# Down-projection of a decoder block: two weight sums made in memory early on, one product added up on another's banks, last sums in another order

## The chip, the cores and the metric

The kernel runs on one core of a Trainium2 chip. The metric is device time in microseconds, the median of several executions. Beside it stands one execution taken by the hardware profiler, whose trace gives every instruction of the engines: TensorE (PE for its matmuls, PEld for its weight loads), VectorE (DVE), ScalarE (ACT), GpSimd (POOL) and SyncE (SP, which here only issues transfers).

## The reference

One layer of a hybrid decoder: attention and an RWKV-7 mixer, merged, then a gated MLP with a causal convolution. 512 tokens, width 1024, MLP width 2816, everything float32. The parts that matter here:

```python
def rwkv7_mixer(p_in, ...):
    ...
    def step(state, inp):
        r_t, w_t, k_t, v_t, a_t, b_t = inp
        sa = jnp.einsum('bhij,bhj->bhi', state, a_t)
        state = state * w_t[:, :, None, :] + sa[..., None] * b_t[:, :, None, :] + v_t[..., None] * k_t[:, :, None, :]
        return state, jnp.einsum('bhij,bhj->bhi', state, r_t)
    ...
def compress_blocks(kv, pe, w1, w2):
    ...
    return jax.nn.gelu(flat @ w1) @ w2
def conv_ffn(h, w_up, conv_w, conv_b, w_down):
    u = h @ w_up
    ...
    val, gate = jnp.split(c, 2, axis=-1)
    return (jax.nn.silu(gate) * val) @ w_down
```

## The kernel before, in words

The program is one long stream that keeps TensorE fed. Each fp32 product is made as three products of rounded parts: a weight tile `raw` is rounded by ACT to `whi` and the rest `wlo` is left by a subtraction on DVE (`wsplit`, L371). SP loads the weight tiles in a fixed order into three `raw` buffers (`wload`, L342).

The stages in order are these. **Preparation** (`prepare`, with `front`, `receptance` and `values_of` for the four pairs of heads) makes the RWKV vectors `kx`, `rx` and `vx`. Then come the query and key projections. The **recurrence** is a loop over eight chunks `c` of 64 tokens. In each chunk PE makes `X`, DVE copies it to `Xs` (L1101), PE makes `U`, ACT and DVE copy it to `UV`, and PE makes `M` and `Y`. Between these small steps the loop calls `next(fill)`: `fill_chain` puts dense products there, and the pieces of `compress`, the two small MLPs on compressed keys and values. Those MLPs need the weights `cmp_w1`, read in four steps `s4`; some of their blocks are loaded by POOL (`spent_load`, L869 and L871) into tiles that the recurrence has finished with: step 2 into `AB` of chunk 0, step 3 into `BKT` of chunk 0 and `AR` of chunk 1. `compress` also clears the tile `vcb` on POOL (a part of `kc`, L969) before ACT writes into it, norms its result with `kcs` on DVE, and scales `kcd` (a part of `QK`), which PE then transposes (L989). In the loop the order on PE was written by hand. The scheduler ordered the other engines, POOL among them.

After attention, output projection and up-projection comes the **down-projection**, in which the order on all engines is written by hand. It multiplies 2x2 blocks in the Strassen-Winograd way, with seven products P1 to P7 on eight banks of PSUM. The rows of `w_down` come in eleven pairs `g`; a pair has four blocks B11 and B12 (loaded as `b1`), B21 and B22 (as `b2`). Four sums of them are needed, and DVE makes them in place: `sum_13` makes B11+B12 and B12+B22 in `b1`, and `sum_24` makes from these the two in `b2`. Even pairs are loaded by POOL into `cgq` (L1773), odd ones by SP into `raw`. Each sum is then split by ACT (`sum_hi`) and DVE (`sum_lo`). P2 and P1 come first, with weights as they are. Then a loop over the pairs makes P5, P7, P4 and P6; P6 takes over the banks of P1 after ACT has copied them to `u[0]`. Last comes P3, during which DVE adds up the results and stores them, four steps and then the two `ends`, each step needing one more split of a weight tile (`produce`).

Of the kernel before, what the change touches and what calls it, by code (L numbers as in the profile page):

```python
# [10 lines left out]
F32 = mybir.dt.float32  # L11
# [73 lines left out]
def hybrid_block(ctx: ExitStack, tc: tile.TileContext, A: dict, out: bass.AP):  # L85
# [14 lines left out]
    dp = ctx.enter_context(tc.tile_pool(name="dram", bufs=1, space=DRAM))  # L100
    wp = ctx.enter_context(tc.tile_pool(name="w", bufs=1))
    usum = dp.tile([4, 512, 128 * len(SF)], F32, name="usum")

    def pool(name, side="left"):
        cm = tc.tile_pool(name=name, bufs=1, side=side)
# [131 lines left out]
    def sums_in_memory(lead=3):  # L237
# [4 lines left out]
        for n in range(len(todo) + lead):  # L242
# [5 lines left out]
            if n >= lead:  # L248
# [2 lines left out]
                                    up_rows(*src, k) if type(src) is tuple else usum[src][128 * k:128 * k + 128],  # L251
                                    accum_op=ALU.add, max_dma_last_dim=2048)

    def weight_tiles():
        def cols(w, o, kt=KT, eng=v):
            return w[:, o:o + 128], kt, 128, eng

        def rows(w, o, n, kt=KT, eng=v):
            step = 1024 // n
            for i, k0 in enumerate(range(0, kt, step)):  # L260
                kn = min(step, kt - k0)
                yield w[128 * k0:128 * (k0 + kn), o:o + n], kn, n, eng[i] if type(eng) is list else eng

        def down_rows(e, c0, order=DOWN):
            src = A["w_down"][0].rearrange("(g e p) n -> e p g n", e=2, p=128)[e]
            for gs in order:
                yield src[:, gs[0]:gs[-1] + 1, c0:c0 + 512], len(gs), 512, v

        pool_ = nc.gpsimd
        yield cols(w_in, O_RWKV + 1536, eng=pool_)  # L270
        yield cols(w_in, O_RWKV + 1664, eng=pool_)
        for p in range(NH2):
            for o in (512, 0, 1024):
                yield cols(w_in, O_RWKV + o + 128 * p)
        yield cols(w_in, O_KC)
        yield from rows(w_in, O_Q, 512, eng=[v, pool_, ("spare", pool_), v])
        yield cols(w_in, O_VC)
        yield from rows(w_in, O_KS, 256, eng=[v, ("spare", v)])
        for m in range(NGA):
            yield cols(w_in, O_GA + 128 * m)  # L280
        yield from rows(w_in, O_KW, 280, eng=pool_)
        for m in range(NGA, KT):
            if m == NGA:
                yield A["cmp_w1_k"][0][0:512], 4, 256, None
                yield A["cmp_w1_v"][0][0:512], 4, 256, None
            elif m < 4:
                yield A["cmp_w1_v"][0][512 * m:512 * m + 512], 4, 256, None
            yield cols(w_in, O_GA + 128 * m)
        for m in range(NGB):
            yield cols(w_in, O_GB + 128 * m)  # L290
        for m in range(KT):
            if m + NGB < KT:
                yield cols(w_in, O_GB + 128 * (m + NGB))
            yield cols(A["w_proj_b"][0], 128 * m, NH2)
        for m in range(KT):
            yield cols(A["w_proj_a"][0], 128 * m, NH2)
        yield from rows(A["w_out"][0], 0, 512)
        yield from rows(A["w_out"][0], 512, 512, eng=())
        for f in range(SF[0]):
            yield cols(A["w_up"][0], DFF + 128 * f)  # L300
            yield cols(A["w_up"][0], 128 * f)
        stream = []
        for f in list(SF) + [None]:
            p = SF[-1] if f is None else f - 1
            if f is not None:
                stream += [up_block(f, 0, 0), up_block(f, 1, 0)]
            if f != SF[0]:
                stream.append(up_sum(p, TS4))
            if f is not None:
                stream.append(up_sum(f, TS2))  # L310
            if f != SF[0]:
                stream.append(up_block(p, 1, 1))
            if f is not None:
                stream += [up_sum(f, TS1), up_sum(f, TS3)]
        yield stream[:1], 4, 128, v
        for i in range(1, len(stream) - 2, 2):
            yield stream[i:i + 2], KT, 128, v
        yield cols(A["w_up"][0], DFF + 128 * (SF[-1] + 1))
        yield stream[-2:], KT, 128, v
        for f in range(SF[-1] + 1, NF):  # L320
            if f != SF[-1] + 1:
                yield cols(A["w_up"][0], DFF + 128 * f)
            yield cols(A["w_up"][0], 128 * f)
        yield from down_rows(1, 0)
        yield from down_rows(0, 0, DOWN_)
        for g in range(1, NG, 2):
            yield A["w_down"][0][256 * g:256 * g + 128], 1, D, "sum"
            yield A["w_down"][0][256 * g + 128:256 * g + 256], 1, D, "sum"
        yield from down_rows(1, 512)

# [245 lines left out]
    def front(p):  # L576
        kx = t2("kx", 2)
        shift_mix(dense_fm(hh, hl), 4 + p, kx)
        L[p]["kx"] = kx

    def rates(p):
        cs = slice(128 * p, 128 * p + 128)
# [39 lines left out]
    def receptance(p):  # L622
        rx = t2("rx", 2)
        shift_mix(dense_fm(hh, hl), p, rx)
        L[p]["rx"] = rx

    def values_of(p):
        vx = t2("vx")
        shift_mix(dense_fm(hh, hl), 8 + p, vx)
        L[p]["vx"] = vx  # L630

    def values_tok(p):
        vx = L[p]["vx"]
# [76 lines left out]
                yield  # L710

    steps = prepare()
    with tc.manual_schedule(engines={mybir.EngineType.PE}):
        next(steps)
        kcp = dense_fm(hh, hl)
    run(steps)
# [369 lines left out]
                mm(U[hsl(r), 64 * p:64 * p + 64], AB[hsl(r), c, p, r, 0:64], Xs[hsl(r), p], True, True)  # L1086
                yield

    with tc.manual_schedule(engines={mybir.EngineType.PE}):
        M0 = Ys = gn = None  # L1090
        X = pb()
        run(x_own(0, X))
# [1 line left out]
        for c in range(NCH):  # L1094
# [4 lines left out]
                spent_load(3, 0)  # L1099
            Xs = tp.tile([128, NH2, DH], F32, name="Xs", tag="Xs", bufs=2)  # L1100
            v.tensor_copy(Xs, X[:, 0:256].rearrange("p (a d) -> p a d", d=DH))  # L1101
            next(fill, None)
            U = pb()
            if c < NCH - 1:
# [630 lines left out]
    ring = xr.tile([128, 2, 2, 2, 512], F32R, name="ring", tag="hl2")  # L1735
    sraw = cgq[:, 0:8].rearrange("p (r a) n -> p r (a n)", r=2)

    def product(banks, x, w, first=False, end=False, ts_=(0, 1)):

        for n, (x_, y) in enumerate(((x[0], w[0]), (x[1], w[0]), (x[0], w[1]))):  # L1740
            for t in ts_:
                mm(banks[t], x_[:, 128 * t:128 * t + 128], y, first and n == 0, end and n == 2)

    def res(t, c, n=512, c0=0):
        return x1[:, t, 512 * c + c0:512 * c + c0 + n]
# [19 lines left out]
    def sum_load(g):  # L1765
        if g >= NG:
            return
        if g % 2:
            raws[g] = [loads.pop(0)[0][:, 0] for _ in range(2)]
        else:  # L1770
            raws[g] = [sraw[:, i] for i in range(2)]
            for i in range(2):
                nc.gpsimd.dma_start(raws[g][i], A["w_down"][0][256 * g + 128 * i:256 * g + 128 * i + 128])  # L1773

    def sum_13(g):
        if g < NG:
            b1, b2 = raws[g]
            tt(b1[:, 0:512], b1[:, 0:512], b1[:, 512:1024], ALU.add)
            tt(b1[:, 512:1024], b1[:, 512:1024], b2[:, 512:1024], ALU.add)

    def sum_24(g):
        if g < NG:
# [26 lines left out]
    with tc.manual_schedule(engines=everything):  # L1809
# [4 lines left out]
        for i, gs in enumerate(DOWN):  # L1814
            w = ahead.pop(0)
            produce()
            if i == 4:
                reload(0, 0, nc.sync)
            elif i == 5:
                sum_13(0)  # L1820
            for j, g in enumerate(gs):
                product(P2, split[N2][g], [x[:, j] for x in w], g == 0, g == NG - 1)
        for i, gs in enumerate(DOWN_):
# [3 lines left out]
            if i == 0:  # L1827
                h13 = sum_hi(0, 0)
                sum_24(0)
            elif i == 1:  # L1830
                h24 = sum_hi(0, 1)
                T[0] = [sum_lo(0, 0, *h13)]
            elif i == 2:
                T[0].append(sum_lo(0, 1, *h24))
                sum_load(2)
            elif i == 3:
                two_parts(a2a[:, 0, :, 0], a2a[:, 1, :, 0], ql[:, 0:5])
            elif i == 4:
                two_parts(a2b[:, 0, :, 0], a2b[:, 1, :, 0], ql[:, 5:NG])
            elif i == 5:  # L1840
                add_to(0, 0, P2)
                sum_load(1)
                sum_13(1)
            for j, g in enumerate(gs):
                product(P1, (a1[:, 0, g], a1[:, 1, g]), [x[:, j] for x in w], g == 0, g == NG - 1)
        u = [[ql[:, 4 * k + 2 * t:4 * k + 2 * t + 2].rearrange("p a n -> p (a n)") for t in range(2)] for k in range(3)]
# [1 line left out]
        for g in range(NG):  # L1848
            n, last = g + 1, g == NG - 1
            if not last:  # L1850
                if g == 0:
                    act_copy(u[0], P1)
                    P6 = [pa(), pa()]
                h13 = sum_hi(n, 0)
                sum_24(n)
                h24 = sum_hi(n, 1)
# [13 lines left out]
                if g == NG - 2:  # L1870
                    two_parts(a1[:, 0, 3:5], a1[:, 1, 3:5], ql[:, 14:16])
                    two_parts(a1[:, 0, 5:7], a1[:, 1, 5:7], cgq[:, 8:10])
                sum_13(g + 2)
            else:
                produce()
                produce()
# [2 lines left out]
            for p, x, w in ((P5, D1, t1), (P7, D3, t3))[::-1 if last else 1]:  # L1879
                product(p, split[x][g], w, g == 0, last)  # L1880
            product(P4, A22p[g], t4, g == 0, last)
            product(P6, split[N2][g], t2, g == 0, last)
        act_copy(u[2], P7)
        add_to(1, 0, u[2])
        add_to(1, 1, u[2], ALU.subtract)
        P3 = [pb(), pb()]
        for i, gs in enumerate(DOWN[:-2]):
            w = ahead.pop(0)
# [2 lines left out]
            if i == 0:  # L1891
                add_to(1, 0, P4)
            elif i == 1:
                for t in range(2):
                    tt(u[0][t], u[0][t], P6[t], ALU.add)
                add_to(1, 0, u[0], eng=nc.gpsimd)
            elif i == 2:
                for t in range(2):
                    tt(u[1][t], u[0][t], P5[t], ALU.add)
            elif i == 3:  # L1900
                store(1, 0, nc.sync)
            produce()
        add_to(0, 1, u[1], ALU.subtract)
# [40 lines left out]
```

## Time and profile before

| | us |
|---|---|
| median of 3 runs | 801.0 (800.76 to 801.12) |
| profiled execution, device time | 801.39 |
| its span in the trace | 799.6 |
| PE, PEld busy in the span | 788.0, 669.3 |
| DVE, ACT, POOL busy | 643.7, 484.6, 93.1 |
| recurrence, first `Xs` to last | 175.60 to 265.78 |
| loop over pairs in the down-projection, first matmul | 718.93 |
| P3, first and last matmul | 779.17 and 795.34 |

The device time is 1.8 us more than the span. Times in the trace count from the start of the span. A matmul's end is modelled, so two matmuls overlap in the rows, and where PE is held up is better read from the distance between starts than from busy time.

### The profile page before, as it was taken

Reading aid. Unit: us, or ns where it says so; the run is one execution under the profiler, and the core shown is the slowest. Engines: PE = TensorE matmul, PEld = TensorE weight load, DVE = VectorE, ACT = ScalarE, POOL = GpSimd, SP = SyncE. Lnnn points to the kernel's source line nnn. Section 1 sums busy time; section 2 is a strip of 40 time slices with the busy share of each in tenths; the row PEclk is TensorE's granted clock in tenths of the full one; section 3 lists DMA queues with packets and bytes.
Section 4 is the critical chain, followed back from the end, with each engine's and each line's share of the span. In section 5 each row is a group of like instructions: output and inputs, shape, how many; then the busy total and the mean of one; then the engine's idle time right before and its main releaser. Section 6 shows DMA issues by size and latency. Waiting matters only on the chain.

```text
span 799.6 us, 14331 instructions
## 1 busy us (share of the span) xinstructions
PE 788.0 (99%) x5475; PEld 669.3 (84%) x5475; DVE 643.7 (80%) x1184; ACT 484.6 (61%) x935; POOL 93.1 (12%) x126
## 2 busy tenths in 40 slices
PE   7999999999999999999999999999999999999997
PEld 5788888887777887887888888999999888888885
DVE  4688899974565688788675489888898999889997
ACT  6777765554455678777435366777777754553452
POOL 5300021152000052221000100000000000002101
PEclk9999999999999999999999999999999999999999
DMA  7432323337362289999757824666666322685754
GB/s 222 125 86 73 99 70 110 82 106 210 81 127 59 73 235 256 267 261 275 180 201 237 190 106 133 185 185 184 185 183 181 112 80 80 196 300 168 237 173 151
DMA packets 141081, 129.17 MB, mean 162 GB/s; under 512 B 5885, under 2 KB 121780, under 8 KB 140884
## 3 DMA queue, kind: packets, MB, share of 16 engines
q1 hardware_dynamic: 125360, 84.00, 36.7%
q0 software_dynamic: 14592, 41.71, 19.8%
q10 hardware_dynamic: 1060, 2.55, 1.0%
q8 instruction: 43, 0.70, 0.4%
q14 instruction: 26, 0.21, 0.1%
HBM read 122.79 MB, written 31.65 MB: 193 GB/s over the span
## 4 chain that ended last, share of the span: by engine, by line
PE 95%; DVE 2%; ACT 2%; DMA 1%; issue 0%; DVEq 0%
PE ps_mm L125 61%; PE ps_mm L1626 9%; PE ps_a L125 8%; PE ps_b L125 5%; PE ps_b L1626 4%; PE ps_a L1626 2%; PE ps_b L1357 1%; PE ps_mm L1357 1%; ACT P L128 1%; ACT whi L128 1%; DMA kc<-in_consts_dram 1%; DVE raw L131 1%; DVE wlo L371 0%; PE ps_b L409 0%; PE ps_b L668 0%
## 5 line engine op out<-in xcount | busy, mean ns | idle before, releaser
L128 ACT ACTIVATE whi<-raw 128x1024 fp32r<-128x1024 f32 (+2 forms) x150 | 149.3, 996 | 128.3 <-PE ps_mm L125 56.4
L371 DVE TENSOR_TENSOR wlo<-raw,whi 128x1024 fp32r<-128x1024 f32 (+1 forms) x135 | 154.7, 1147 | 42.7 <-ACT whi L128 25.1
L125 PE MATMUL ps_mm<-hh,whi 128*128 128x512 f32 (+1 forms) x416 | 161.5, 391 | 0.3 <-ACT whi L128 0.2
L125 PE MATMUL ps_mm<-hl,whi 128*128 128x512 f32 (+1 forms) x416 | 154.2, 382 | 0.0
L125 PE MATMUL ps_mm<-hh,wlo 128*128 128x512 f32 (+1 forms) x416 | 103.9, 382 | 0.0
L125 PEld LDWEIGHTS ps_mm<-hh,whi 128*128 128x128 f32 x416 | 78.2, 188 | 17.7 <-issue 0.8
L125 PEld LDWEIGHTS ps_mm<-hh,wlo 128*128 128x128 f32 x416 | 78.1, 188 | 15.5 <-DVE wlo L371 0.3
L125 PEld LDWEIGHTS ps_mm<-hl,whi 128*128 128x128 f32 x416 | 76.2, 188 | 14.5 <-DVE hl L140 0.3
L1773 POOL DMA_DIRECT2D cgq<-in_w_down_dram x12 | 6.4, 537 | 289.1 <-DVE cgq L131 236.5
L128 ACT ACTIVATE P<-P,nm 128x512 f32<-128x512 f32 (+3 forms) x64 | 35.3, 553 | 6.5 <-DVE nm L1320 6.4
L131 DVE TENSOR_TENSOR cgq<-cgq 128x512 f32<-128x512 f32 (+1 forms) x49 | 32.8, 670 | 1.6 <-DMA cgq<-in_w_down_dram 0.8
L140 DVE SCALAR_TENSOR_TENSOR cgq<-cr,cw,cgq 128x511 f32<-128x511 f32 (+1 forms) x38 | 28.4, 748 | 5.4 <-ACT cgq L128 5.0
L1320 DVE CUSTOM_DVE_ANT_0 P<-ps_a,AB 128x512 f32<-128x512 f32 (+3 forms) x64 | 29.3, 483 | 2.6 <-PE ps_a L125 2.6
L140 DVE SCALAR_TENSOR_TENSOR cgq<-ps_mm,cw,cgq 128x511 f32<-128x511 f32 (+1 forms) x36 | 26.2, 742 | 0.8 <-ACT cgq L128 0.7
L1626 PE MATMUL ps_mm<-hl,whi 128*128 128x256 f32 x104 | 26.1, 283 | 0.0
L1626 PE MATMUL ps_mm<-hh,whi 128*128 128x256 f32 x104 | 26.1, 283 | 0.0
L128 ACT ACTIVATE ring<-cgq 128x1024 fp32r<-128x1024 f32 x12 | 12.7, 1061 | 16.5 <-DVE cgq L131 16.1
L128 ACT ACTIVATE QK<-ps_mm 128x64 f32<-128x64 f32 (+5 forms) x52 | 13.4, 304 | 15.3 <-PE ps_mm L125 15.2
L125 PE MATMUL ps_mm<-whi,hh 128*128 128x280 f32 (+2 forms) x72 | 22.4, 331 | 0.0
L125 PE MATMUL ps_mm<-whi,hl 128*128 128x280 f32 (+2 forms) x72 | 21.9, 323 | 0.0
L125 PE MATMUL ps_mm<-obT,whi 128*128 128x512 f32 x64 | 20.1, 397 | 0.0
L1626 PEld LDWEIGHTS ps_mm<-hl,whi 128*128 128x128 f32 x104 | 20.0, 192 | 0.1
(540 smaller groups left out, 1951.0 us busy)
## 6 DMA issues: line engine op xcount, KB each, us to landing
usum<-in_w_up_dram POOLq DMA_DIRECT2D x24, 832.0 KB, 26.5
raw<-in_w_in_dram SPq DMA_DIRECT2D x38, 512.0 KB, 3.8
raw<-usum SPq DMA_DIRECT2D x52, 256.0 KB, 3.4
raw<-in_w_down_dram SPq DMA_DIRECT2D x25, 512.0 KB, 4.7
raw<-in_w_up_dram SPq DMA_DIRECT2D x39, 256.0 KB, 3.6
raw<-in_w_up_dram SPq DMA_DIRECT2D x18, 512.0 KB, 3.8
usum<-usum POOLq DMA_DIRECT2D x8, 832.0 KB, 23.1
cgq<-in_w_down_dram POOLq DMA_DIRECT2D x12, 512.0 KB, 4.5
```

What stands on the lines that cost most here:

```text
L125: te.matmul(o, lhsT=l, rhs=r, start=start, stop=stop)
L128: sc.activation(o, i, f, **kw)
L131: v.tensor_tensor(o, a, b, op=op)
L140: v.scalar_tensor_tensor(o, a, s, b, op0=op0, op1=op1)
L371: eng.tensor_tensor(lo, raw, hi.bitcast(F32), op=ALU.subtract)
L1320: v.tensor_tensor_reduce(out=P[:, b, r], in0=sp[:, r - r0, b], in1=BT[:, h, 384 - 128 * qt:512], scale=-1.0, scalar=-NEG, op0=ALU.add, op1 ...
L1357: te.transpose(pt[:, 128 * i:128 * i + 128], P[:, x, i, 128 * k:128 * k + 128], ident)
L1626: te.matmul(bank_, lhsT=(hi, lo)[k // 4][:, k % 4], rhs=y[:, k % 4], start=first and k == 0 and y is x[0], stop=k == 7, skip_group_check=n ...
L1773: nc.gpsimd.dma_start(raws[g][i], A["w_down"][0][256 * g + 128 * i:256 * g + 128 * i + 128])
```

## The change

A tile `dsum` in DRAM holds, for each pair, the two sums that `sum_13` made. POOL's transfers make it: `down_copy` copies `b1`'s rows into it, one pair at a time, and `down_add` adds B12 and B22 to its two halves by accumulating transfers. They are tied to the program by `after`: a one-element copy on POOL (`hold`) that reads a result, so that the transfer behind it isn't issued sooner. The eleven copies hang on `kx`, `rx` and `vx` in the preparation, and the eleven adds on `Xs` of chunks 0 to 5, two at a time. For this POOL's order is now the written one in the preparation and in the recurrence. In the down-projection `sum_13` is gone and `b1` is loaded from `dsum`.

The product P6 is no longer made on cleared banks and added by DVE: its matmuls go on adding to P1's banks after ACT has copied P1 out, and ACT copies the sum out at the end of the loop. Some of the last sums stand later or earlier.

```diff
+    dsum = dp.tile([NG, 128, D], F32, name="dsum")
...
+    def after(result):
+        hold = tp.tile([128, 1], F32, name="hold", tag="hold")
+        nc.gpsimd.tensor_copy(hold[0:1], result)
+    def down_copy(g):
+        nc.gpsimd.dma_start(dsum[g], A["w_down"][0][256 * g:256 * g + 128], max_dma_last_dim=2048)
+    def down_add(g):
+        nc.gpsimd.dma_start(dsum[g].rearrange("p (e n) -> p e n", e=2),
+                            A["w_down"][0][256 * g:256 * g + 256, 512:1024].rearrange("(e p) n -> p e n", e=2),
+                            accum_op=ALU.add, max_dma_last_dim=2048)
+    def down_sums():
+        for g in range(NG):
+            after((yield))
+            down_copy(g)
+        for g in range(0, NG, 2):
+            after((yield))
+            for g_ in range(g, min(g + 2, NG)):
+                down_add(g_)
...
-            yield A["w_down"][0][256 * g:256 * g + 128], 1, D, "sum"
+            yield dsum[g], 1, D, "sum"
...
+        memory_down.send(kx[0:1, 0:1])
...
-    with tc.manual_schedule(engines={mybir.EngineType.PE}):
+    with tc.manual_schedule(engines={mybir.EngineType.PE, mybir.EngineType.Pool}):
         next(steps)
...
             v.tensor_copy(Xs, X[:, 0:256].rearrange("p (a d) -> p a d", d=DH))
+            memory_down.send(Xs[0:1, 0, 0:1])
             next(fill, None)
...
-    def sum_13(g):
-        if g < NG:
-            b1, b2 = raws[g]
-            tt(b1[:, 0:512], b1[:, 0:512], b1[:, 512:1024], ALU.add)
-            tt(b1[:, 512:1024], b1[:, 512:1024], b2[:, 512:1024], ALU.add)
...
                 if g == 0:
                     act_copy(u[0], P1)
-                    P6 = [pa(), pa()]
...
-            product(P6, split[N2][g], t2, g == 0, last)
+            product(P1, split[N2][g], t2, False, last, more=True)
         act_copy(u[2], P7)
-        add_to(1, 0, u[2])
-        add_to(1, 1, u[2], ALU.subtract)
+        act_copy(u[0], P1)
...
             elif i == 1:
-                for t in range(2):
-                    tt(u[0][t], u[0][t], P6[t], ALU.add)
                 add_to(1, 0, u[0], eng=nc.gpsimd)
-            elif i == 2:
                 for t in range(2):
                     tt(u[1][t], u[0][t], P5[t], ALU.add)
+            elif i == 2:
+                add_to(1, 0, u[2])
             elif i == 3:
+                add_to(1, 1, u[2], ALU.subtract)
                 store(1, 0, nc.sync)
```

The sequence of matmuls on PE is the same before and after but for buffer and line numbers. Three places where other engines' instructions stand otherwise follow. In the changed kernel most line numbers are 1 to 35 higher.

**POOL in chunk 0 of the recurrence.** The first rows are of before, from the last split of a key weight on; `QK<-QK,kss` scales the keys, `QK<-QK,qss` the queries, `AB`, `BKT` and `AR` are the loads for the compression's steps 2 and 3.

```order
L371 TENSOR_TENSOR wlo<-raw,whi 128x560
L839 TENSOR_TENSOR QK<-QK,kss 128x128 x4
L912 TENSOR_TENSOR QK<-QK,qss 128x512 x4
L869 DMA BKT<-in_cmp_w_k_dram 128x256 x2
L871 DMA AB<-in_cmp_w_k_dram 128x4x256
L839 TENSOR_TENSOR QK<-QK,kss 128x128 x4
L869 DMA AR<-in_cmp_w_k_dram 128x2x128 x2
```

The same place in the changed kernel, to the adds of chunk 1.

```order
L400 TENSOR_TENSOR wlo<-raw,whi 128x560
L872 TENSOR_TENSOR QK<-QK,kss 128x128 x4
L945 TENSOR_TENSOR QK<-QK,qss 128x512 x4
L259 COPY hold<-Xs 1x1
L265 DMA dsum<-in_w_down_dram 256x1x512 x2
L872 TENSOR_TENSOR QK<-QK,kss 128x128 x4
L904 DMA AB<-in_cmp_w_k_dram 128x4x256
L902 DMA BKT<-in_cmp_w_k_dram 128x256 x2
L902 DMA AR<-in_cmp_w_k_dram 128x2x128 x2
L259 COPY hold<-Xs 1x1
L265 DMA dsum<-in_w_down_dram 256x1x512 x2
```

The load into `AB` stood ahead of the second scaling of keys, and now stands behind it, and behind a hold and two adds.

**POOL, the clearing of `vcb`** (`MEMSET kc`). Before, it stood long ahead of the recurrence, beside the clearing of the tile `inv`.

```order
L371 TENSOR_TENSOR wlo<-raw,whi 128x1024
L869 DMA BKT<-in_cmp_w_v_dram 128x256
L969 MEMSET kc 128x256
L734 MEMSET inv 128x1024
L735 MEMSET inv 128x32
```

In the changed kernel it stands in chunk 4, its written place; the rows begin at the hold of chunk 3 and end at that of chunk 5.

```order
L259 COPY hold<-Xs 1x1
L265 DMA dsum<-in_w_down_dram 256x1x512 x2
L259 COPY hold<-Xs 1x1
L265 DMA dsum<-in_w_down_dram 256x1x512 x2
L1002 MEMSET kc 128x256
L259 COPY hold<-Xs 1x1
L265 DMA dsum<-in_w_down_dram 256x1x512
```

It moved behind the hold and the two adds of chunk 4, and ACT's copies into `vcb` wait for POOL there, which they did not before.

**DVE in chunk 4.** `rs_y` and `kcs` are the steps of the reciprocal root for the compressed keys, `QK<-QK,kcs` scales them for PE's transposition, `M` is the state. The rows of before begin at the second step of the root.

```order
L131 TENSOR_TENSOR rs_y<-kcs 32x2
L140 SCALAR_TENSOR_TENSOR rs_y<-rs_y,rs_m 32x2
L140 SCALAR_TENSOR_TENSOR kcs<-rs_y,kcs 32x2
L131 TENSOR_TENSOR rs_y<-kcs 32x2
L140 SCALAR_TENSOR_TENSOR rs_y<-rs_y,rs_m 32x2
L140 SCALAR_TENSOR_TENSOR kcs<-rs_y,kcs 32x2
L135 TENSOR_SCALAR QK<-QK,kcs 32x64 x4
L1110 COPY UV<-ps_b 64x4x64
L371 TENSOR_TENSOR wlo<-raw,whi 128x1024
L131 TENSOR_TENSOR M<-M,ps_a 128x256
L131 TENSOR_TENSOR M<-M,PC 128x256
```

In the changed kernel the copy of `UV` stands ahead of the root's first step; from the second step on the rows are these.

```order
L132 TENSOR_TENSOR rs_y<-kcs 32x2
L141 SCALAR_TENSOR_TENSOR rs_y<-rs_y,rs_m 32x2
L141 SCALAR_TENSOR_TENSOR kcs<-rs_y,kcs 32x2
L400 TENSOR_TENSOR wlo<-raw,whi 128x1024
L132 TENSOR_TENSOR rs_y<-kcs 32x2
L132 TENSOR_TENSOR M<-M,ps_a 128x256
L141 SCALAR_TENSOR_TENSOR rs_y<-rs_y,rs_m 32x2
L132 TENSOR_TENSOR M<-M,PC 128x256
L141 SCALAR_TENSOR_TENSOR kcs<-rs_y,kcs 32x2
L136 TENSOR_SCALAR QK<-QK,kcs 32x64 x4
```

The split of a weight tile and the two steps of the state now stand ahead of the scaling, which was first.

More of the change, by code (lines that the diff above doesn't have):

```diff
@@ L252, in sums_in_memory @@
                                     accum_op=ALU.add, max_dma_last_dim=2048)
+    def after(result):
[15 more added lines that the diff above has]
+                down_add(g_)
+        while True:
+            yield
+    memory_down = down_sums()
+    next(memory_down)
     def weight_tiles():
@@ L625, in receptance @@
         L[p]["rx"] = rx
+        memory_down.send(rx[0:1, 0:1])
     def values_of(p):
@@ L630, in values_of @@
         L[p]["vx"] = vx
+        if p + 1 < NH2:
+            memory_down.send(vx[0:1, 0:1])
     def values_tok(p):
@@ L1087, in through @@
                 yield
-    with tc.manual_schedule(engines={mybir.EngineType.PE}):
+    with tc.manual_schedule(engines={mybir.EngineType.PE, mybir.EngineType.Pool}):
         M0 = Ys = gn = None
@@ L1736, in hybrid_block, with product @@
     sraw = cgq[:, 0:8].rearrange("p (r a) n -> p r (a n)", r=2)
-    def product(banks, x, w, first=False, end=False, ts_=(0, 1)):
+    def product(banks, x, w, first=False, end=False, ts_=(0, 1), more=False):
         for n, (x_, y) in enumerate(((x[0], w[0]), (x[1], w[0]), (x[0], w[1]))):
             for t in ts_:
-                mm(banks[t], x_[:, 128 * t:128 * t + 128], y, first and n == 0, end and n == 2)
+                te.matmul(banks[t], lhsT=x_[:, 128 * t:128 * t + 128], rhs=y, start=first and n == 0,
+                          stop=end and n == 2, skip_group_check=more)
     def res(t, c, n=512, c0=0):
@@ L1771, in sum_load @@
             raws[g] = [sraw[:, i] for i in range(2)]
-            for i in range(2):
-                nc.gpsimd.dma_start(raws[g][i], A["w_down"][0][256 * g + 128 * i:256 * g + 128 * i + 128])
-    def sum_13(g):
-        if g < NG:
-            b1, b2 = raws[g]
-            tt(b1[:, 0:512], b1[:, 0:512], b1[:, 512:1024], ALU.add)
-            tt(b1[:, 512:1024], b1[:, 512:1024], b2[:, 512:1024], ALU.add)
+            for i, s_ in enumerate((dsum[g], A["w_down"][0][256 * g + 128:256 * g + 256])):
+                nc.gpsimd.dma_start(raws[g][i], s_)
     def sum_24(g):
@@ L1818, in hybrid_block @@
                 reload(0, 0, nc.sync)
-            elif i == 5:
-                sum_13(0)
             for j, g in enumerate(gs):
@@ L1842, in hybrid_block @@
                 sum_load(1)
-                sum_13(1)
             for j, g in enumerate(gs):
@@ L1872, in hybrid_block @@
                     two_parts(a1[:, 0, 5:7], a1[:, 1, 5:7], cgq[:, 8:10])
-                sum_13(g + 2)
             else:
```

## The prediction

> **What bounds the kernel now.** I read the page's busy times first, then PE's weight loads among the waits of the last 100 us, then the timeline there, because the change is aimed at the down-projection.
>
> ```profile
> PE 788.0 (99%) x5475; PEld 669.3 (84%) x5475; DVE 643.7 (80%) x1184; ACT 484.6 (61%) x935; POOL 93.1 (12%) x126
> PEld ps_b L125 <- DVE wlo L371: 1.9, 4, 0.8
> 718.93 1.52 PE L125 MATMUL ps_mm<-ring,d1a_pairs 128*128 128x512 f32 x6
> 720.29 1.52 PE L125 MATMUL ps_b<-ring,d3a_pairs 128*128 128x512 f32 x6
> 779.17 1.07 PE L125 MATMUL ps_b<-whi,a 128*128 128x512 f32 x4
> 795.34 0.39 PE L125 MATMUL ps_b<-wlo,a 128*128 128x512 f32 x1
> ```
>
> PE is the bound: it is hardly ever without work, so any stall of PE, at any place, goes straight onto the time, and any work taken from DVE counts only as far as PE waited for it. Six matmuls start 1.36 us after the six before (720.29 less 718.93), so one takes 0.2267. The loop over pairs has 264 of them, 59.84 us; it took 60.24 (to 779.17), so 0.40 is lost. P3 has 66, whose last would start 14.73 after the first; it starts 16.17 after, so 1.44 is lost. **All that the down-projection can give back is 1.84 us**, and DVE's late `wlo` is what the waits show for it.
>
> **Part one: the sums leave DVE.**
>
> ```profile
> L131 DVE TENSOR_TENSOR cgq<-cgq 128x512 f32<-128x512 f32 (+1 forms) x49 | 32.8, 670 | 1.6 <-DMA cgq<-in_w_down_dram 0.8
> 779.80 2.49 DVE L1750 TENSOR_TENSOR x1b<-x1b,ql 128x512 f32<-128x512 f32 x4
> 780.28 1.07 ACT L128 ACTIVATE whi<-raw 128x1024 fp32r<-128x1024 f32 x1 [1.30 <-PE ps_b L125]
> 783.41 1.22 DVE L371 TENSOR_TENSOR wlo<-raw,whi 128x1024 fp32r<-128x1024 f32 x1
> 784.68 0.74 PE L125 MATMUL ps_b<-wlo,a 128*128 128x512 f32 x2 [0.36 <-DVE wlo L371]
> 789.43 1.06 ACT L128 ACTIVATE whi<-raw 128x1024 fp32r<-128x1024 f32 x1 [1.98 <-PE ps_b L125]
> 791.81 0.50 PE L125 MATMUL ps_b<-wlo,a 128*128 128x512 f32 x1
> 785.74 1.95 DVE L371 TENSOR_TENSOR wlo<-raw,whi 128x1024 fp32r<-128x1024 f32 x1
> ```
>
> `sum_13` is 22 additions of 0.67 us, 14.7 us of DVE; the loop's lost 0.40 should go with it, the rest of the 14.7 lay beside PE. In P3, DVE did four sums (2.49) ahead of its first split, so `wlo` came at 783.41 and PE stalled to 784.68. With them moved to later steps, and the two additions of P6 gone, that split can follow its `whi` (780.28 + 1.07), and the stall there and the next go. ACT's two new copies of P1 (about 0.5 each) fit into its 1.30 of idleness ahead of 780.28. The last split can't be hidden: ACT may begin only when the fourth step's weights are free (789.43), PE gets it 2.38 later (791.81) and has only eight matmuls, 1.81, to do meanwhile. About 0.6 of the 1.44 stays, with the sums now standing closer before it. POOL's long addition now falls beside an earlier split, which would take 1.95 as at 785.74 and not 1.22; it still ends before its weights are wanted. If these covers fail, 0.7 returns. Gain: 0.40 + 1.44 - 0.6 = **1.2 us**, between 0.5 and 1.8. Nothing is gained or lost on PE by adding P6 up on P1's banks: matmuls and order are the same.
>
> **Part two: POOL's transfers.** The eleven copies hang on vectors of the preparation.
>
> ```profile
> 56.76 1.23 DVE L371 TENSOR_TENSOR wlo<-raw,whi 128x1024 fp32r<-128x1024 f32 x1 [0.87 <-ACT whi L128]
> 76.08 1.06 ACT L128 ACTIVATE whi<-raw 128x1024 fp32r<-128x1024 f32 x1 [0.54 <-PE ps_mm L125]
> raw<-in_w_proj_b_dram SPq DMA_DIRECT2D x7, 256.0 KB, 11.1
> ```
>
> A `raw` buffer freed at 58.0 is read at 76.1, three tiles on: a weight load has 18 us there. Even beside the stream of `usum`, where a load took 11.1 to land, it would be in time. I cost the copies at nothing; that stream is the cover's test, and the hold itself is one element on an engine that was idle there.
>
> **Part three: the load into `AB` moves behind the keys' scaling.** This is the first large term.
>
> ```profile
> 175.84 4.04 POOL L912 TENSOR_TENSOR QK<-QK,qss 128x512 f32<-128x512 f32 x4
> 185.04 0.76 POOL L871 DMA_DIRECT2D AB<-in_cmp_w_k_dram  x1
> 189.31 1.48 POOL L839 TENSOR_TENSOR QK<-QK,kss 128x128 f32<-128x128 f32 x4 [3.50 <-DVE kss L140]
> 193.16 0.43 PE L125 MATMUL ps_mm<-AB,sg 128*64 128x256 f32 x1
> sg<-in_cmp_w_k_dram POOLq DMA_DIRECT2D x1, 512.0 KB, 4.2
> AB<-in_cmp_w_k_dram POOLq DMA_DIRECT2D x1, 512.0 KB, 5.8
> 178.82 0.45 SPq L342 DMA_DIRECT2D raw<-in_w_in_dram  x1
> 184.20 1.06 ACT L128 ACTIVATE whi<-raw 128x1024 fp32r<-128x1024 f32 x1 [0.99 <-DMA raw<-in_w_in_dram]
> ```
>
> `AB` was issued at 185.04 and landed 5.8 later, at 190.8; PE wanted it at 193.16. Now POOL first waits for `kss` (DVE, no earlier than 189.3) and scales the keys, so it issues at 189.31 + 1.48 = 190.8. The two 512 KB loads of this kind took 4.2 and 5.8: it lands at 195.0 to 196.6, and PE, whose order is fixed, stalls 1.8 to 3.4. Queued behind it on POOL are the loads for step 3 and all later adds; step 3 comes some 9 us later on PE and takes no harm.
>
> The two adds of chunk 0 are issued just after 179.9 (175.84 + 4.04), while a weight load issued at 178.82 is in flight, on whose landing ACT begins at 184.20. If they share its last 2 us, it is up to 2.2 late (my estimate, the rest of its transfer at half speed); ACT's work for `kss` stands behind it, so `AB` shifts by as much. The term is 1.8 to 5.6. I take 0.5 of lateness and a landing of 5.0: 196.3 against 193.16, **3.1 us**.
>
> [...]
>
> **Part four: the clearing of `vcb` and the scaling in chunk 4.** The second large term.
>
> ```profile
> 229.65 0.41 DVE L1101 COPY Xs<-ps_b 128x256 f32<-128x256 f32 x1
> 229.37 0.90 ACT L128 ACTIVATE kc<-ps_mm 32x64 f32<-32x64 f32 x4 [0.15 <-PE ps_mm L125]
> 232.90 0.38 ACT L128 ACTIVATE UV<-ps_b 64x256 f32<-64x256 f32 x1 [1.80 <-PE ps_b L125]
> 291.93 1.34 POOL L250 DMA_DIRECT2D usum<-in_w_up_dram  x1 [3.48 <-DMA usum<-in_w_up_dram]
> 309.42 0.99 POOL L250 DMA_DIRECT2D usum<-usum  x1 [6.52 <-DMA usum<-in_w_up_dram]
> 117.91 0.34 POOL L969 MEMSET kc<- 128x256 f32 x1
> 233.90 0.73 DVE L135 TENSOR_SCALAR QK<-QK,kcs 32x64 f32<-32x64 f32 x4
> 235.90 1.22 DVE L371 TENSOR_TENSOR wlo<-raw,whi 128x1024 fp32r<-128x1024 f32 x1 [0.81 <-ACT whi L128]
> 237.15 0.42 DVE L131 TENSOR_TENSOR M<-M,ps_a 128x256 f32<-128x256 f32 x1
> 236.81 0.31 PE L989 MATMUL ps_mm<-kc,QK 32*128 32x32 f32 x2
> ```
>
> The clearing waits for `Xs` (230.06), a hold (about 0.2, an estimate below the clearing's 0.34) and two issues of adds; these cost 0.99 or 1.34 for `usum`, and I take 0.99 because that form has rows of 512 elements too. With 0.34 for the clearing it ends at 232.6. ACT's copies into `vcb` then begin 3.2 later than at 229.37. They and what follows took until 231.1 (232.90 less 1.80), 1.7 us, so `kcs` can start at about 234.35, and ACT's `UV` and `whi` queue behind, 1.5 late, still in time for PE. DVE then does two small steps, `UV` (0.43), six more steps of 0.18 (0.73 over four), the split (1.22), three steps, the state (2 x 0.42) and the scaling (0.73): 234.35 + 0.36 + 0.43 + 1.1 + 1.22 + 0.55 + 0.85 + 0.73 = 239.6. PE wants the scaled keys at 236.81: **2.8 us**. Were ACT not late at all, the split would still start at 235.90 and the new order give 239.2, 2.4; with issues of 1.34, 3.5.
>
> **Sum**, against the profiled execution's 801.39: + 3.1 + 2.8 - 1.2 = + 4.7, 806.1. The median shown is 0.39 below that execution, so **805.7**. PE has no idle stretch afterwards in which the two stalls could be absorbed. Bounds of this case: + 1.8 + 2.4 - 1.8 = 2.4 to + 5.6 + 3.5 - 0.5 = 8.6, 803.4 to 809.6.
>
> **Rivals.**
> 1. Not slower: both waits are covered and only the gain is left. Its place is POOL in chunk 0: it decides by the landing of `AB`, which must come within 2.4 us of issue, and by DVE finishing the scaling at 236.8. Against it: 4.2 is the shortest landing of such a load. Time 801.0 - 1.2 = 799.8, at best 799.2.
> 2. Only one of the two waits reaches PE (a short landing, or work of DVE that slips forward when PE is late): + 1.7 or so, 802.7.
> 3. The adds also delay weight loads in later chunks. For it: each pair of adds is 1 MB at the pace of a chunk; against it: only in chunk 0 does ACT wait for a load. Three more stalls of 1.5 (the 2.2 of lateness, less about 0.7 of slack on ACT, both my estimates) bring 810.2.
>
> That the sums don't leave DVE is no rival: its order shows two additions for each pair where four stood.
>
> **Chances.** Forecast 0.63, rival 1 0.10, rival 2 0.17, rival 3 0.10. A difference under 0.2%, 1.6 us, can't be told from none. Faster by more (below 799.4): half of rival 1, 0.05. Within: its other half and half of rival 2, 0.05 + 0.09 = 0.14. Slower: 0.81. The range 802.0 to 809.4 leaves out rival 1, most of rival 3 and a little of rival 2.
>
> **What would show it.** In the changed trace PE's first matmul on `AB` starts about 3 us after its neighbours and names a transfer; POOL's load into `AB` is issued after its keys' scaling; in chunk 4 ACT's copy into `kc` waits for POOL and PE's transposition of `QK` for DVE. In the down-projection 264 matmuls take under 60.0 and P3 loses about 0.6. Stalls of under 1 us at both places, or weight loads on which ACT waits in the preparation, would make it wrong.

## The result, and the profile after

The changed kernel is slower: the ratio to the kernel before is 1.0089 (95% interval 1.0075 to 1.0102), five executions of 806.6 to 809.3 us, median 808.4, against a median of 801.0. One further execution, of 878.94, was disturbed and the ratio leaves it out. The profiled execution took 809.26, its span is 807.4, so 7.8 more than the 799.6 of before; all that follows splits up these 7.8.

The same view of before was read first for what PE waited for. These two waits are new among PE's waits in the changed kernel (engine, line, what it waited for: total, times, longest).

```profile
PE ps_mm L1022 <- DVE QK L136: 2.8, 1, 2.8
PE ps_mm L126 <- DMA AB<-in_cmp_w_k_dram: 2.5, 1, 2.5
```

They are the two waits that were forecast. The timeline of the first place, on POOL and PE, with the landing of the load from the list of transfers:

```profile
184.22 1.06 ACT L129 ACTIVATE whi<-raw 128x1024 fp32r<-128x1024 f32 x1 [1.02 <-DMA raw<-in_w_in_dram]
189.29 1.47 POOL L872 TENSOR_TENSOR QK<-QK,kss 128x128 f32<-128x128 f32 x4 [7.23 <-DVE kss L141]
190.72 0.84 POOL L904 DMA_DIRECT2D AB<-in_cmp_w_k_dram  x1
195.75 0.43 PE L126 MATMUL ps_mm<-AB,sg 128*64 128x256 f32 x1 [2.53 <-DMA AB<-in_cmp_w_k_dram]
199.07 0.63 PE L126 MATMUL ps_mm<-hh,whi 128*128 128x512 f32 x1
199.50 0.63 PE L126 MATMUL ps_mm<-hl,whi 128*128 128x512 f32 x1
...
AB<-in_cmp_w_k_dram POOLq DMA_DIRECT2D x1, 512.0 KB, 5.0
```

The load was issued at 190.72 and PE's matmul started at 195.75, 2.59 later than at 193.16 before. But the two last rows of PE show something that was not forecast: these matmuls start 0.43 us apart, where one of the same shape took 0.2267 before. The granted clock was half there. Each row is one stretch of the recurrence: its length, busy times of PE, PEld, DVE, ACT and POOL with instructions, and behind them PE's granted clock, the share of the DMA engines and GB/s.

```profile
193.71:197.12 3.41, 1.37 (x14) 0.94 (x16) 1.65 (x2) 1.84 (x4) 2.58 (x4) 1.00 0.92 270
197.12:200.54 3.42, 3.42 (x12) 2.19 (x9) 0.00 (x0) 0.00 (x0) 0.00 (x0) 0.50 1.00 182
241.49:244.91 3.42, 1.07 (x5) 0.92 (x6) 2.67 (x11) 0.97 (x3) 0.00 (x0) 1.00 1.13 219
244.91:248.32 3.41, 3.41 (x9) 2.68 (x9) 0.00 (x1) 0.00 (x0) 0.00 (x0) 0.50 1.03 232
```

PE was busy for only 1.37 and 1.07 us of the 3.41 in which most of each stall fell, and through the next 3.41 its clock was half. The second stretch begins 47.79 us after the first (244.91 less 197.12), which is 14 times 3.413, the length of each stretch in the trace's record of the clock. By these rows (0.43 us a matmul for 0.2267, a clock of 0.50 for 1.00) PE did in 3.41 us about half of what it does at the full clock, so up to 1.7 us are lost behind each stall; matmul by matmul against before, 1.57 was lost behind the first and 1.51 behind the second.

The second place, chunk 4, on POOL, ACT, DVE and PE:

```profile
234.37 0.19 POOL L259 COPY hold<-Xs 1x1 f32<-1x1 f32 x1 [9.87 <-DVE rs_m L138]
234.83 2.10 POOL L265 DMA_DIRECT2D dsum<-in_w_down_dram  x2 [0.27 <-issue]
235.94 1.31 POOL L1002 MEMSET kc<- 128x256 f32 x1
237.29 0.89 ACT L129 ACTIVATE kc<-ps_mm 32x64 f32<-32x64 f32 x4 [3.90 <-POOL kc L1002]
239.06 0.16 DVE L138 TENSOR_SCALAR rs_m<-kcs 32x2 f32<-32x2 f32 x1 [2.01 <-ACT QK L129]
240.92 1.22 DVE L400 TENSOR_TENSOR wlo<-raw,whi 128x1024 fp32r<-128x1024 f32 x1
243.22 0.73 DVE L136 TENSOR_SCALAR QK<-QK,kcs 32x64 f32<-32x64 f32 x4
243.84 0.41 PE L1022 MATMUL ps_mm<-kc,QK 32*128 32x32 f32 x2 [2.77 <-DVE QK L136]
```

This is the chain that was forecast: the clearing stands behind the hold and two issues, ACT's copies wait for the clearing, the root of the keys on DVE for ACT, DVE does the split ahead of the scaling, and PE waits for the scaling. The clearing's row, 1.31 long, begins while the second issue is still under way (234.83 + 2.10 = 236.93) and ends 0.32 behind it, so nothing shows the clearing itself to have cost more than the 0.34 it took in the preparation. PE's transposition stands 7.02 later than before; 4.16 it had brought from the first place, so 2.86 are this stall.

The down-projection, on ACT and PE: the split of a weight tile in the loop of P1, the first matmul of the loop over pairs, and the first and last of P3.

```profile
714.33 1.06 ACT L129 ACTIVATE whi<-raw 128x1024 fp32r<-128x1024 f32 x1 [2.85 <-DMA raw<-in_w_down_dram]
728.17 1.07 PE L1776 MATMUL ps_mm<-ring,d1a_pairs 128*128 128x512 f32 x4
788.01 1.07 PE L1776 MATMUL ps_b<-whi,a 128*128 128x512 f32 x4
803.19 0.39 PE L1776 MATMUL ps_b<-wlo,a 128*128 128x512 f32 x1
```

The loop takes 59.84 (788.01 less 728.17), exactly 264 times 0.2267: the 0.40 is gained. P3 takes 15.18 where it took 16.17: 0.99 is gained. But in the loop of P1 a weight tile landed late in this execution (714.33), which cost PE 0.69. The account is 2.59 + 1.57 + 2.86 + 1.51 + 0.69 - 0.40 - 0.99 = 7.83, and the spans differ by 7.84.

### The profile page after: what moved, and what is told of

Read it like the earlier page. It is cut to its first block, busy times and chain, and to the rows that moved or that the text cites. A ratio compares the mean times of both kernels' runs of the same rounds, so it can differ in the third digit from the quotient of the medians.

```text
span 807.4 us, 14367 instructions
## 1 busy us (share of the span) xinstructions
PE 791.3 (98%) x5475; PEld 672.5 (83%) x5475; DVE 629.4 (78%) x1160; ACT 484.4 (60%) x937; POOL 115.4 (14%) x165
## 4 chain that ended last, share of the span: by engine, by line
PE 92%; DMA 3%; ACT 2%; DVE 2%; issue 0%; POOL 0%; DVEq 0%; SPq 0%; ACTq 0%; POOLq 0%
PE ps_mm L126 54%; PE ps_mm L1660 9%; PE ps_mm L1776 5%; PE ps_b L1660 4%; PE ps_a L126 4%; PE ps_b L1776 3%; PE ps_a L1776 3%; PE ps_a L1660 2%; PE ps_b L126 2%; PE ps_b L1391 1%; DMA raw<-in_w_down_dram 1%; ACT whi L129 1%; DVE wlo L400 1%; PE ps_mm L1391 1%; DMA raw<-in_w_in_dram 1%; DMA AB<-in_cmp_w_k_dram 1%
## 5 line engine op out<-in xcount | busy, mean ns | idle before, releaser
L126 PE MATMUL ps_mm<-hh,whi 128*128 128x512 f32 (+1 forms) x416 | 163.4, 396 | 0.3 <-ACT whi L129 0.2
L126 PE MATMUL ps_mm<-hl,whi 128*128 128x512 f32 (+1 forms) x416 | 156.0, 387 | 0.0
L1808 POOL DMA_DIRECT2D cgq<-dsum x6 | 3.3, 542 | 275.0 <-DVE cgq L132 236.5
L132 DVE TENSOR_TENSOR cgq<-cgq 128x512 f32<-128x512 f32 (+1 forms) x37 | 24.6, 665 | 1.0 <-DMA cgq<-in_w_down_dram 0.5
```

The source lines that it names most:

```text
L126: te.matmul(o, lhsT=l, rhs=r, start=start, stop=stop)
L132: v.tensor_tensor(o, a, b, op=op)
L1808: nc.gpsimd.dma_start(raws[g][i], s_)
```

## The experiments

Three questions were open: whether the two stalls stem from the order on POOL, whether the half clock belongs to the stalls, and what is left without them. PE's order is that of before in all of them but e8 and e10, where a few matmuls at the end of the up-projection swap places. The kernel before ran beside them with medians of 800.81 (e1 to e4), 800.89 (e5, e7, e8, e9) and 800.64 (e10, e11).

| run | what it is | median us | ratio (95%) |
|---|---|---|---|
| e1 | changed, `AB` ahead of the key scaling | 806.40 | 1.0069 (1.0052 to 1.0085) |
| e2 | changed, `vcb` cleared early | 804.11 | 1.0040 (1.0025 to 1.0055) |
| e3 | both | 801.19 | 1.0006 (0.9997 to 1.0015) |
| e4 | before, last sums and P6 only | 800.47 | 0.9995 (0.9985 to 1.0004) |
| e5 | before, POOL's written order only | 803.39 | 1.0035 (1.0022 to 1.0048) |
| e7 | both, nine adds in the preparation | 800.17 | 0.9990 (0.9981 to 0.9999) |
| e8 | before, five long stalls | 836.41 | 1.0442 (1.0423 to 1.0461) |
| e9 | e2, `AB` behind one scaling of four | 802.16 | 1.0016 (1.0007 to 1.0025) |
| e10 | before, short stalls | 811.09 | one execution |
| e11 | e3 with DVE's sums, tile not read | 801.53 | 1.0008 (0.9999 to 1.0017) |

**The load into AB ahead of the scaling (e1).**

```diff
         if b == 1:
-            norm_keys(1)
+            rstd(kss[:, 1].rearrange("p t h -> p (t h)"), DH)
...
     def norm_keys(b):
-        rstd(kss[:, b].rearrange("p t h -> p (t h)"), DH)
+        if b == 0:
+            rstd(kss[:, 0].rearrange("p t h -> p (t h)"), DH)
...
                 spent_load(2, 0)
+                norm_keys(1)
```

> The changed kernel, but the load into AB is issued ahead of the second scaling of keys again (behind the hold and two adds of chunk 0). In the changed kernel's trace PE waited 2.59 us for this load, and 1.4 us later the granted clock was half for 3.41 us, in which PE lost another 1.57. Theory (the stall also brings the half clock): both go, 4.2 us off, about 804.2, and the clock is half only once in the recurrence. Rival 1 (the half clock has another cause): only 2.6 off, 805.8, clock still half twice. Rival 2 (the traffic of the added transfers costs the time): no change, about 808.4.

PE no longer waits for `AB`, and the clock is half once only. Yet the run is 2.2 above the theory. A new wait shows why: a weight tile lands late in chunk 1, ACT rounds it late, DVE's split and copy of `Xs` come after, and PE waits for `Xs`. The rows are of ACT and PE, then the weight loads between 184 and 206 us of this kernel and of the kernel before.

```profile
206.04 1.06 ACT L129 ACTIVATE whi<-raw 128x1024 fp32r<-128x1024 f32 x1 [5.91 <-DMA raw<-in_w_in_dram]
209.34 0.27 PE L126 MATMUL ps_b<-Xs,AB 64*64 64x64 f32 x1 [1.63 <-DVE Xs L1135]
...
raw<-in_w_in_dram SPq DMA_DIRECT2D x3, 512.0 KB, 8.9
```

```profile
raw<-in_w_in_dram SPq DMA_DIRECT2D x5, 512.0 KB, 4.4
```

The median landing is 8.9 us beside the adds and 4.4 without them. In the changed kernel the stall at `AB` had hidden this. So the third rival of the prediction, adds that delay weight loads, is real too, though only once the larger stalls are gone. And the stall of 1.63 here is followed by no half clock:

```profile
205.15:208.56 3.41, 2.56 (x12) 1.76 (x10) 1.43 (x2) 2.49 (x4) 0.00 (x0) 1.00 0.04 12
208.56:211.97 3.41, 2.63 (x41) 2.19 (x42) 3.07 (x16) 0.79 (x3) 2.27 (x3) 1.00 0.75 196
```

With the time cut into stretches of 3.41 us, counted in steps from the half clock of chunk 4 (windows, from here on), it falls on two of them, and PE is busy for 2.56 and 2.63 in these.

**The clearing of vcb early (e2).**

```diff
     vcb = kc[:, 128:384].rearrange("p (b d) -> p b d", d=DH)
+    nc.gpsimd.memset(vcb, 0.0)
...
     def compress():
...
-        nc.gpsimd.memset(vcb, 0.0)
```

> The changed kernel, but vcb is cleared before the recurrence, so that it doesn't stand behind the hold and the adds of chunk 4, and the scheduler puts the scaling of the compressed keys ahead of the split again. Theory: the stall of 2.86 us and the 1.51 us that the half clock behind it cost both go, 4.4 off, about 804.0. Rival 1 (half clock of another cause): 805.5. Rival 2 (traffic): about 808.4.

As the theory had it, 804.11: the stall in chunk 4 and its half clock are gone together, the other pair is there (PE waits 2.5 for `AB`). DVE's order in chunk 4 is that of before again.

**Both (e3).**

> Both edits, the rest as in the changed kernel, with all its transfers. Theory: 8.5 off, no half clock before the end, and what the down-projection gains (0.55 of P3 and loop, net of a new 0.7 in the loop of P1) is left: about 800.0, 0.1 to 0.2% below the kernel before. Rival 1: 803.1 with a half clock in the recurrence. Rival 2 (traffic): above 804.

There is no half clock ahead of the program's end, and no wait of PE above 0.6 us behind the start. Of the 8.5 all but 1.2 come off; the median is 801.19, no different from before. Its executions spread more, 800.75 to 803.08, than those of before (800.40 to 801.48). The load into `AB`, issued at 184.84, took 8.4 to land, and matmul by matmul against before PE has lost 0.7 by 207 us in the profiled execution, the fastest of the ten.

**Only the last part of the change (e4).**

> The kernel before with only the last part of the change: P6 added up on the banks of P1 and the last sums in the new order; the four sums of weights stay on DVE and no transfer is added. Theory (the gain of P3, 0.9, comes from the shorter row of sums on DVE ahead of its first splits): P3 loses 0.5 instead of 1.44, total 800.1. Rival (it comes from the sums of weights that DVE no longer makes): 801.0 as before.

800.47, 0.3 under the kernel before, which its interval doesn't tell from none. Its trace says more: P3 takes 15.24 and the loop over pairs 60.20. So what P3 gains (0.93 of 0.99) belongs to the order of the last sums and to P6, and what the loop gains (0.4) to the sums of weights that DVE no longer makes. The other traces say how firm this is. The loop takes 59.84 in all six kernels that read the tile and 60.20 to 60.25 in the six that don't. P3 varies more: 15.7 to 16.2 in the four kernels with the old order of the last sums (before, e5, e8, e10), 15.2 to 15.4 in the eight with the new. Its gain is real, but its size, of 0.2 to 1.0, isn't known from one execution of each.

**POOL's order alone (e5).** The kernel before with `Pool` added to the two engine sets of the diff.

> The kernel before with one thing of the change: POOL's order in preparation and recurrence is the written one; no tile in DRAM, no added transfers, no holds. Theory (the load into AB is late because its written place is behind the second scaling of keys, whatever else POOL does): the stall of 2.6 us and a half clock behind it, together 4.1, so about 804.9; the clearing of vcb finds POOL idle, so no stall in chunk 4. Rival (the holds and adds ahead of it on POOL make it late): no stall, 801.0.

The stall is there without any hold, add or tile: the load's written place behind the scaling makes it. The median is 1.5 below the forecast, since most executions show no half clock.

```profile
PE ps_mm L125 <- DMA AB<-in_cmp_w_k_dram: 2.1, 1, 2.1
```

And there is none in chunk 4. Its five executions fall into two kinds: spans of 802.9 and 803.5 with a mean clock of 0.998, and 801.4, 801.6 and 801.6 with 1.000. One half clock of 3.41 us is 0.002 of a mean over 800. So the stall here, 2.1 us in the profiled execution, seems sometimes to halve the clock and sometimes not, and the two kinds lie 1.3 to 2.1 apart; the stalls of the others weren't traced. The changed kernel's executions show the same: 807.4, 806.6 and 806.9 with 0.996, 0.996 and 0.995, but 806.1 and 804.8 with 0.998.

**A shorter stall (e9).** In e2, three of the four scalings stand behind the load.

> The changed kernel with vcb cleared early (which alone gave 804.11) and with the load into AB issued behind one of the four key scalings instead of all four, 1.1 us sooner. Theory (a stall of 1.6 us had no half clock behind it in the first experiment, one of 2.3 to 2.9 had): the stall shrinks from 2.5 to about 1.4 and the half clock goes with it, so 1.1 + 1.6 off, 801.4. Rival (the half clock belongs to the place, not to the length of the stall): only 1.1 off, 803.0, clock still half once.

The profiled execution has a stall of 1.55 and no half clock. The median fell by 1.95, more than the 1.0 by which the stall shrank, less than the 2.7 forecast; weight loads in the recurrence still land late (0.35 at 211 us). The theory holds for the clock of this execution, and its size was too good. One of the ten, 803.79, has a mean clock of 0.998, as with one half clock; its stall wasn't traced.

**Stalls elsewhere (e8).** On the kernel before, ACT repeats the rounding of five weight tiles of the up-projection.

```diff
                     act(hi, raw)
+                    splits[0] += 1
+                    for _ in range({66: 3, 76: 4, 86: 5, 96: 6, 106: 7}.get(splits[0], 0)):
+                        act(hi, raw)
```

> The kernel before with nothing of the change; at five weight tiles of the up-projection, far apart, ACT makes the rounded part 3, 4, 5, 6 and 7 times more than needed (1.06 us each), so that PE waits. Theory: five stalls of about 0.7, 1.7, 2.8, 3.8 and 4.9 us (each repeat less some 2.5 of lead); behind the last three the granted clock is half for 3.41 us or a multiple, which begins a whole number of 3.41 us after any other such stretch; behind the first two it isn't. Total about 801 + 13.9 + 3 x 1.6 = 820. Rival (the half clock comes from the recurrence's small matmuls or the accumulating transfers): no half clock here, 815.

The stalls (from the end of one matmul to the start of the next) came out longer than reckoned, 2.04, 3.27, 5.38, 6.84 and 7.50, so none was small, and the total is 16 above the forecast. All five are followed by half clock: one window behind the first two, two behind the others. The second of the two came even behind 567.43 to 570.85, a window at half clock with only 1.03 idle. The window of the shortest and the next:

```profile
495.75:499.17 3.42, 1.38 (x12) 1.18 (x11) 1.75 (x4) 3.42 (x5) 0.00 (x0) 1.00 0.30 90
499.17:502.58 3.41, 3.41 (x19) 3.41 (x18) 2.33 (x3) 0.13 (x1) 0.00 (x0) 0.50 0.43 128
```

The five stretches begin at 499.17, 533.30, 567.43, 604.98 and 642.53, steps of 10, 10, 11 and 11 times 3.413. There is no recurrence here and no accumulating transfer: the rival is out.

**Short stalls (e10).** The same tiles, with part of the width repeated where a whole one was too long.

> As the experiment with repeated splits on the kernel before, but with shorter repeats (2.75, 2.75, 1.7, 1.5 and 1.7 us of added work of ACT at the same five tiles), so that the stalls come out at some 1.6 to 2.0 us. So far every window of 3.41 us (counted from the first rise of the clock) in which PE was idle for 2.04 us or more was followed by a window of half clock, and none with 1.50 or less. Theory (what counts is idle time within one window, with a bound between 1.50 and 2.04): a stall that two windows share never halves the clock, one that lies in a single window does if it is over the bound, so some of the five and not all. Rival (the length of the stall alone counts, bound between 1.6 and 2.0): those of one length behave alike, however the windows lie. Total about 801 + 9 + 1.6 for each half clock, 810 to 818.

Three stalls of size came out, 1.62, 1.63 and 1.85, each within one window. Only the last has a half clock behind it:

```profile
590.34 0.39 PE L1631 MATMUL ps_mm<-hh,whi 128*128 128x256 f32 x1 [1.85 <-ACT whi L128]
...
587.58:590.99 3.41, 1.56 (x13) 1.36 (x12) 2.50 (x5) 2.71 (x5) 0.00 (x0) 1.00 0.48 143
590.99:594.40 3.41, 3.41 (x18) 3.41 (x18) 1.97 (x3) 1.20 (x2) 0.00 (x0) 0.50 0.47 127
```

With the other traces, windows at the full clock with 1.85, 2.04, 2.04, 2.12, 2.34, 2.50, 2.52 and 2.77 us idle were followed by half clock, and those with 1.63 or less were not. By these windows, a bound on idle time would lie between 1.63 and 1.85 us of 3.41. The ends of the programs, where PE runs out of work, narrow it: behind a last window with 2.29 to 2.77 idle (e3, e4, e7, e8) the next was at half clock, behind one with 1.70 (e5) or 1.84 (e2) it wasn't. The rows are of e2.

```profile
796.87:800.29 3.42, 1.58 (x7) 0.95 (x6) 1.33 (x3) 0.00 (x0) 0.00 (x0) 1.00 0.75 277
800.29:803.70 3.41, 0.00 (x0) 0.00 (x0) 0.00 (x0) 0.00 (x0) 0.00 (x0) 1.00 0.09 30
```

As the ends of matmuls are modelled, 1.84 and 1.85 can't be told apart: by these traces the bound would be near 1.85, which is an estimate from the windows named here. No stall of over 1.7 was shared by two windows so that neither came near the bound, so the profiles don't tell idle time in a window from the length of a stall; only the two kinds of executions in e5 and in the changed kernel, whose stalls weren't all traced, hint at the window.

**The transfers without their use (e11).**

> The kernel with both mends and all 22 transfers in their places, but the down-projection reads the blocks of w_down as before and DVE makes all four sums, so the tile in DRAM is made and not used; the last part of the change (P6 on the banks of P1, order of the last sums) is in. Beside the kernel with that last part alone (800.47) it has only the transfers and POOL's order more. Theory (the transfers in the recurrence cost 1.0, the sums that leave DVE bring back 0.3): 801.5. Rival (the transfers cost nothing, reading the tile in the down-projection does): 800.5.

801.53 against e4's 800.47, beside kernels before of 800.64 and 800.81: the transfers and POOL's order, mended, cost 1.1 to 1.2 us. In its trace PE loses 0.9 of this between 198 and 212 us; weight loads between 184 and 206 us land in 7.4 us in the median, and ACT waits 4.38 us for one.

**The adds in the preparation (e7).** As e3, with this order of the transfers:

```diff
             down_copy(g)
+            if g >= 2:
+                down_add(g - 2)
...
-        for g in range(0, NG, 2):
+        for _ in range(4):
+            yield
+        for g in range(NG - 2, NG):
             after((yield))
-            for g_ in range(g, min(g + 2, NG)):
-                down_add(g_)
+            down_add(g)
```

> Both mends (AB ahead of the keys' scaling, vcb early), and nine of the eleven adds issued in the preparation, each behind the copy two pairs later, the last two on Xs of chunks 4 and 5. Theory (what keeps the kernel with both mends at 801.2 instead of 800.0 is adds in the recurrence that make weight loads and the load into AB land late, 8.4 us instead of 5.8 there): 799.7, and its runs spread less. Rival (the 1.2 has its cause in the down-projection or in reading the tile in DRAM): 801.0 as with the adds in the recurrence.

800.17, faster than the kernel before by 0.09% (interval 0.01 to 0.19), with executions from 799.79 to 800.54. Weight loads land in time again; the rows are of this kernel's loads between 184 and 206 us.

```profile
raw<-in_w_in_dram SPq DMA_DIRECT2D x5, 512.0 KB, 5.0
AB<-in_cmp_w_k_dram POOLq DMA_DIRECT2D x1, 512.0 KB, 5.8
```

In the preparation, where a weight load has 18 us (58.0 to 76.1 in the rows of before), the same adds delay nothing that PE feels: its longest wait behind the start is 0.7. This is the version that beats both kernels, by the full 0.40 in the loop (59.84) and 0.73 in P3 (15.44). From e4, which has the last sums alone and no transfer, it can't be told: 0.9981 to 0.9999 of the kernel before against 0.9985 to 1.0004. So what the sums made in memory bring by themselves is seen in the loop's 0.40 of each trace, and not shown in the medians.

## Why the prediction was right, and where it was short

**Direction, places and order of the waits** were right: slower, by PE waiting for `AB` in chunk 0 and for the scaled keys in chunk 4, each by the chain that was named. e2, e3 and e5 show the causes: take the written place of the load or of the clearing away and its stall goes; give POOL the written order alone and the first stall comes.

**The load into AB**: 3.1 forecast, 2.59 measured. The issue (190.72 against 190.8) and the landing (5.0) were as taken. The 0.5 of lateness of ACT, the author's estimate for transfers that share a landing, is shown by no run: its `whi` began at 184.22, where it began at 184.20 before, and at 184.11 to 184.15 in e1, e2 and e3, which have the same adds.

**The clearing**: 2.8 forecast, 2.86 measured, from two errors that cancel, which is luck. From the end of `Xs` (234.23) to the first issue it took 0.60, where the hold was reckoned at 0.2, and the two issues took 2.10 and not 1.98, so ACT began 0.5 later than reckoned; the clearing itself, 0.32, was as taken. DVE's steps from there on overlapped more, 4.8 from the first step of the root to PE's transposition instead of 5.2.

**The gain**: 1.2 forecast, 1.39 measured (0.40 and 0.99, the second of which varies, as e4 showed), less 0.69 for a weight load that landed late in the loop of P1. None of the five other profiles of kernels that read the tile there (e1, e2, e3, e7, e9) has that stall, so it isn't a fixed part of the change; why that load was late stays open.

**The step that failed** is the first one, "any stall of PE, at any place, goes straight onto the time", and with it the sum. The stalls of 2.59 and 2.86 cost more than themselves: behind each PE's clock was half for 3.41 us, 1.57 and 1.51 us more. The sum of the stalls and the gain as forecast, 4.7, lacked these 3.1; the measured excess is 7.1 us by the ratio (0.0089 of 801) and 7.8 in the profiled execution. That 4.7 and 3.1 add up to those 7.8 is luck: the stalls came out 0.45 shorter and the gain 0.19 larger than forecast, and the late load's 0.69 made up for both. The result stayed within the range only because its upper end was set by longer stalls, which didn't happen; that is luck too.

**The rivals.** The first (both covered) and the second (one of them) are out. The third (adds delay weight loads) has no part in the result that could be shown, since the stalls gave the loads time, but it is what held e3 and e11 at 1.0 to 1.2 above what they could be, and e7 took it away.

## What to carry to other kernels

Price a new stall of PE, where PE bounds, as its length plus what the clock does behind it: behind the stalls of 2.59 and 2.86 us here the second part was 1.57 and 1.51, and behind those of 1.63 (e1) and 1.55 (e9) the clock stayed full. When an engine's order is taken from a scheduler and written by hand, look at everything else that the scheduler had pulled forward on that engine: here a load and a clearing, neither of which the change was about, made two stalls that outweigh everything else in the account. And give transfers that nobody waits for a stage in which the loads that somebody waits for have slack.

## What the runs showed of the hardware

- PE's clock was half for stretches of 3.41 us (3.413 in the record of the changed kernel's clock), which began whole steps of that length apart: 14 in the changed kernel (47.79 us), 10, 10, 11 and 11 in e8 (34.13, 34.13, 37.55 and 37.55). Of the windows at the full clock that are named here, those in which PE was idle for 1.85 us or more were followed by one at half clock and those with 1.84 or less were not, the ends of the programs included. Behind the stalls of 5.38, 6.84 and 7.50 us of e8 the half clock lasted two windows; that execution's mean clock was 0.983.
- One kernel had two times: e5 took 801.4 to 801.6 or 802.9 to 803.5 us of span with the same instructions, at a mean clock of 1.000 or 0.998.
- Rows of POOL overlapped, so a row's length wasn't always its cost: the clearing of 128x256 had a row of 0.34 us in the preparation of the kernel before and of 1.31 in chunk 4 of the changed one, but there it began while a transfer's issue ahead of it was under way and ended 0.32 behind that.
- A weight load of 512 KB landed in 4.4 us in the median between 184 and 206 us of the kernel before, and in 8.9 in e1, beside accumulating transfers of 512 KB, which took 9.5 themselves.
